# A hybrid decoder layer: token-major convolution products, and a state space that begins later and takes some steps on neighbouring weight pieces

## The chip, the cores and the metric

The kernel runs on one core of a Trainium2 chip. The metric is the device time of one execution in microseconds (us), the lower the better. An execution of the kernel before takes 1211.44 us (median of 3 runs, 1211.16 to 1211.69).

## The reference

One layer of a decoder with three mixers and a gated merge, for 256 tokens and a model width of 2048, all in float32:

```python
h = rms_norm(x, norm_w)
sb_q, sb_k, sb_v, sb_z, ssd_z, ssd_xbc, ssd_dt, mem_q, mem_z, gate_pre = split(h @ w_in)
o_sb  = stick_breaking_attention(sb_q, sb_k, sb_v) * silu(sb_z)
xbc   = silu(causal_depthwise_conv(ssd_xbc, conv_w, conv_b))     # 4096 channels, 4 taps
x_ssm, b_in, c_in = split(xbc)                                   # 2048, 1024, 1024
dt    = softplus(ssd_dt + dt_bias)
y     = ssd_chunked_scan(x_ssm, dt, -exp(a_log), b_in, c_in)     # 8 groups of 4 heads
o_ssd = group_rms_norm((y + d_skip * x_ssm) * silu(ssd_z))
o_mem = memory_cross_attention(mem_q, rms_norm(mem), w_mem_kv) * silu(mem_z)
gates = sigmoid(gate_pre + b_gate)
merged = g_sb * (o_sb @ w_branch_sb) + g_ssd * (o_ssd @ w_branch_ssd) + g_mem * (o_mem @ w_branch_mem)
out = rms_norm(x + merged @ w_out, final_norm_w)
```

## The kernel before

**Weight pieces.** All large products go through `gemm` (L249) or `gemm_cols` (L211). Weights are read once, in pieces of 512 KB (a tile `raw`, loaded by SyncE's queue). `split` (L142) makes two fp32r tiles of a piece: ScalarE (ACT) copies it to `wh` (L146), and VectorE (DVE) writes the rest, `wl = raw - wh` (L150). Three products in fp32r stand for one in fp32: high x high, high x low, low x high. There are three `wh` and three `wl` buffers, so the copy of a piece may start when TensorE (PE) has finished the piece three before it. In `gemm` a piece is 12 matmuls, 512 columns wide (L269 to L271), and the result lies token-major in PSUM, 128 tokens to a tile. In `gemm_cols` a piece is 8 matmuls 512 wide (L229, the high weights on both halves of the input at once) and 8 of 256 (L233), and the result lies channel-major.

**Side work.** After each piece `pump` (L185) issues the rest of the kernel: first the steps whose due piece has come (`defer`), then one step of one of two lanes, the even pieces' or the odd pieces'. A step is a Python generator's stretch up to its next `yield`. Every engine runs its instructions in the order in which they were issued, so what `pump` issues after piece n stands ahead of piece n+1's `wh` on ACT, ahead of its `wl` on DVE, and ahead of its matmuls on PE. Pieces are numbered here from the first: values, keys and queries of the memory attention, the z parts and the stick-breaking attention take 1 to 160, the convolution 161 to 224, the gates and projection of branch mem 225 to 272, of branch sb 273 to 320, of branch ssd 321 to 384, the output 385 to 408.

**Results turned by DVE.** Most products of `gemm` are wanted channel-major. `turning` (L301) does it: DVE transposes 32x32 blocks out of PSUM (L308), a DMA takes them to a scratch in DRAM (L313), four DMAs bring them back (L323), and ACT copies the blocks to their place.

**The convolution** (L733 on) uses `gemm_cols`, 16 calls of 4 pieces. `fold` (L239) adds the two halves of the result (ACT L246, DVE L247). Then `taps` does the four taps on DVE: a scaled copy (L745) and three scalar-tensor-tensor operations (L748, STT below). `silu` (L202) is one ACT operation of 128x1024 for four channel tiles. `turn_x` (L755 on) turns x token-major through a scratch again (DVE L764, DMAs L768 and L772), a quarter (two groups) at a time.

**The state space** (`ssd_group`, L813) has 8 groups, the even ones in one lane, the odd ones in the other. It is put into the lanes 4 pieces after the convolution (L933) and runs under the pieces of branches mem and sb. A group's steps are: the decay input by DMA and the products `cb` (PE L825, L826); `xs`, `cbs` (ACT L841) and the masked decays (DVE L844); 6 exponentials of 128x128 (ACT L851); 6 more, and a weighing by `cbs` (DVE L855); two weighings; the products `y` of two groups together (PE L874); the skip and z (DVE L887, L890); the squares (ACT L892), their split, their sum `tot` (PE L900); Ln, Exp, Identity, Square on ACT (L906 to L909); the scaling. After a wait of the lanes the result is split (`ssd_cols`). `finish` (L978) issues whatever is left in the lanes ahead of the first product of branch ssd.

**ACT's function tables.** Exponential and logarithm share one table (`exp_ln`, L804), sigmoid has another (the gates, `sigmoid`, L808), silu a third. `sigmoid` marks the table as gone, so that the next exponential loads it again.

**Gates and branches.** In each branch, for each of four column groups, first the gate's product (8 pieces), then the projection (4 pieces in branches mem and sb, 8 in branch ssd). `gate_evac` adds the bias on DVE (L951) and defers the sigmoid by one piece; `branch_evac` multiplies (L960, L962) and adds on GpSimd (POOL, L963).

Of the kernel before, what the change touches and what calls it, by code (L numbers as in the profile page):

```python
# [10 lines left out]
F32 = mybir.dt.float32  # L11
# [5 lines left out]
P = 128  # L17
# [24 lines left out]
def trunk_kernel(  # L42
# [159 lines left out]
    def silu(a, chunks=LATE):  # L202
        defer(lambda: nc.scalar.activation(a, a, AF.Silu), chunks)
# [529 lines left out]

    cT = [slot([P, 8, T], F32, "cT") for _ in range(4)]

    def conv_evac(i0):
        def evac(acc):
            u = tmp.tile([P, 2, T], F32, tag="cu", name=nm("cu"), bufs=2)
            fold(u, acc)
            for b in range(2):  # L740
                defer(lambda b=b: taps(u[:, b], i0 + b), 1 + 2 * b)

        def taps(u, i):
            a = cT[i // 8][:, i % 8]
            nc.vector.tensor_scalar(a, u, convw[:, 3, i:i + 1], convb[:, i:i + 1], ALU.mult,  # L745
                                    ALU.add)
            for s in range(1, 4):
                nc.vector.scalar_tensor_tensor(a[:, s:T], u[:, 0:T - s],  # L748
                                               convw[:, 3 - s, i:i + 1], a[:, s:T],
                                               ALU.mult, ALU.add)  # L750
# [33 lines left out]
    waiting = [zT[i // 2][:, 4 * (i % 2):4 * (i % 2) + 4] for i in range(4)]
    for i, g in enumerate((4, 5, 6, 7, 0, 1, 2, 3)):
        for j in range(2):
            gemm_cols(hT, NKT, w_in, C_XBC + g * GW + 2 * j * P, conv_evac(4 * g + 2 * j))
        waiting.insert(5 if i == 4 else len(waiting),
                       cT[g // 2][:, 4 * (g % 2):4 * (g % 2) + 4])
        if i >= 4:  # L790
            for j in range(3):
                silu(waiting.pop(0), 6 if not waiting else 1 + j)
        if i == 5:
            defer(lambda: turn_x(0), 5)


    oD = []
    ssd_done = []
    pair = []

    def exp_ln():

        if not tables[0]:
            nc.scalar.preload_act_table_set("natural_log_exp_and_others")  # L804
            tables[0] = True

    def sigmoid(a):
        nc.scalar.activation(a, a, AF.Sigmoid)  # L808
        tables[0] = False

    tables = [False]

    def ssd_group(g):  # L813

        heads = range(4 * g, 4 * g + 4)
        xT = [cT[i // 8][:, i % 8] for i in (2 * g, 2 * g + 1)]
        zg = turned(zT[g // 4], 2 * (g % 4), 2)

# [6 lines left out]
        nc.tensor.matmul(cb[:, 0:2], bT[:, g, 0:P], cTT[:, g], start=True, stop=True)  # L825
        nc.tensor.matmul(cb[:, 2], bT[:, g, P:T], cTT[:, g, P:T], start=True, stop=True)  # L826
        yield
        xs = tb([P, 2, T], "xs")
        rows = x_rows[g // 2]
        for t in range(2):  # L830
            for b in range(2):
                dt2 = dts[:, t, heads[0] + 2 * b:heads[0] + 2 * b + 2]
                nc.vector.tensor_tensor(
                    xs[:, t, b * P:(b + 1) * P].rearrange("p (h i c) -> p h i c", h=2, c=32),
                    rows[:, :, t, 2 * (g % 2) + b].rearrange("p (h i) c -> p h i c", h=2),
                    dt2.unsqueeze(2).unsqueeze(3).to_broadcast([P, 2, 2, 32]), ALU.mult)
# [4 lines left out]
        nc.scalar.activation(cbs, cb, AF.Copy)  # L841
        over = lambda a: a.unsqueeze(1).to_broadcast([P, 4, P])
# [277 lines left out]
```

## Time and profile before

| | |
|---|---|
| median of 3 runs | 1211.44 us |
| the profiled execution | 1211.59 us |
| its span in the trace | 1209.9 us |
| share of the span that PE is busy | 99% (5820 matmuls) |
| DVE, ACT, POOL | 65%, 52%, 4% |
| DMA share in the stretch 469 to 659 us (convolution) | 0.66 |
| granted TensorE clock, mean | 0.998 |

The span is the stretch of the trace from the first to the last instruction; the execution's time is 1.7 us longer. In rows of the timeline the first number is the start in us from the span's beginning, the second the duration; "x3" means that three instructions alike, one behind the other, were put into one row, and brackets at a row's end give the idle time ahead of it and what ended it. Durations of neighbours overlap a little, so what an instruction costs its engine is best read as the distance between two starts.

### The profile page before, as it was taken

The page shows a single profiled execution, that of the slowest core. Times are in us where ns is not written, and L with a number is a line of the kernel's source. Part 1 is how long each engine was busy: PE and PEld are TensorE (multiplying, and loading weights), DVE is VectorE, ACT ScalarE, POOL GpSimd, SP SyncE. Part 2 cuts the span into 40 slices and gives each one's busy share as a digit, 9 for nine tenths or more (in the row PEclk, how much of TensorE's full clock was granted, in tenths as well). Part 3 has the DMA queues.
Part 4 walks back from the last instruction along what each step waited for, and adds up shares of the span by engine and source line. Part 5 has one row for each costly group of instructions (what it writes and reads, how often), then busy time and mean ns, then how long its engine had stood idle before and what let it go on. Part 6 is the DMA issues. An engine that isn't in the chain of part 4 may idle for free.

```text
span 1209.9 us, 15621 instructions
## 1 busy us (share of the span) xinstructions
PE 1199.0 (99%) x5820; PEld 1005.8 (83%) x5820; DVE 791.6 (65%) x1035; ACT 634.1 (52%) x844; POOL 52.5 (4%) x50
## 2 busy tenths in 40 slices
PE   9999999999999999999999999999999999999997
PEld 7888888888888888888888888888888888888886
DVE  5686664546564555888887858677777655556752
ACT  6754443354355444545655756484757534444541
POOL 0100000000000000010100000000000010110101
PEclk9999999999999999999999999999999999999999
DMA  9977787887666777665668676667756677778751
GB/s 320 363 229 228 215 244 235 251 232 214 197 192 194 218 224 226 185 189 169 180 179 261 210 226 214 212 204 220 229 177 202 204 221 222 228 219 293 252 203 70
DMA packets 169820, 264.66 MB, mean 219 GB/s; under 512 B 11984, under 2 KB 67472, under 8 KB 169616
## 3 DMA queue, kind: packets, MB, share of 16 engines
q1 hardware_dynamic: 134304, 227.41, 61.6%
q10 hardware_dynamic: 35440, 36.26, 9.2%
q8 instruction: 45, 0.74, 0.2%
q14 instruction: 31, 0.25, 0.1%
HBM read 249.45 MB, written 14.19 MB: 218 GB/s over the span
## 4 chain that ended last, share of the span: by engine, by line
PE 97%; issue 1%; DMA 1%; ACT 0%; DVE 0%; SPq 0%; POOLq 0%; POOL 0%; ACTq 0%
PE acc L269 25%; PE acc L271 25%; PE acc L270 25%; PE acc L229 10%; PE acc L233 5%; PE acc L457 1%; PE acc L458 1%; PE acc L456 1%; PE y L874 1%; DMA raw<-in_w_mem_kv_dram 1%; PE dtp L518 0%; PE acc L1074 0%; PE acc L1072 0%; PE acc L1073 0%; PE spo L708 0%
## 5 line engine op out<-in xcount | busy, mean ns | idle before, releaser
L150 DVE TENSOR_TENSOR wl<-raw,wh 128x1024 fp32r<-128x1024 f32 (+1 forms) x409 | 504.4, 1236 | 309.4 <-ACT wh L146 307.9
L146 ACT ACTIVATE wh<-raw 128x1024 fp32r<-128x1024 f32 (+1 forms) x409 | 431.4, 1056 | 426.8 <-PE acc L271 337.1
L269 PE MATMUL acc<-wh,hT 128*128 128x512 f32 x896 | 350.9, 392 | 0.0
L270 PE MATMUL acc<-wl,hT 128*128 128x512 f32 x896 | 348.9, 389 | 0.3 <-DVE wl L150 0.3
L271 PE MATMUL acc<-wh,hT 128*128 128x512 f32 x896 | 348.9, 389 | 0.0
L271 PEld LDWEIGHTS acc<-wh,hT 128*128 128x128 f32 x896 | 168.2, 188 | 35.4
L270 PEld LDWEIGHTS acc<-wl,hT 128*128 128x128 f32 x896 | 168.3, 188 | 34.4 <-DVE wl L150 0.7
L269 PEld LDWEIGHTS acc<-wh,hT 128*128 128x128 f32 x896 | 168.3, 188 | 33.9 <-issue 0.3
L229 PE MATMUL acc<-hT,wh 128*128 128x512 f32 x512 | 161.6, 397 | 0.0
L233 PEld LDWEIGHTS acc<-hT,wl 128*128 128x128 f32 x512 | 96.2, 188 | 22.7
L233 PE MATMUL acc<-hT,wl 128*128 128x256 f32 x512 | 100.7, 278 | 0.0
L229 PEld LDWEIGHTS acc<-hT,wh 128*128 128x128 f32 x512 | 78.1, 189 | 0.1
L269 PE MATMUL acc<-wh,oD 128*128 128x512 f32 x128 | 49.8, 389 | 0.0
L270 PE MATMUL acc<-wl,oD 128*128 128x512 f32 x128 | 49.8, 389 | 0.0
L271 PE MATMUL acc<-wh,oD 128*128 128x512 f32 x128 | 49.8, 389 | 0.0
L748 DVE SCALAR_TENSOR_TENSOR cT<-cu,wcols,cT 128x255 f32<-128x255 f32 (+2 forms) x96 | 46.4, 483 | 3.4
L963 POOL TENSOR_TENSOR merged<-merged,sig 128x512 f32<-128x512 f32 x16 | 25.8, 1637 | 512.3 <-DVE sig L962 512.3
L269 PE MATMUL acc<-wh,mT 128*128 128x512 f32 x96 | 37.4, 390 | 0.0
L271 PE MATMUL acc<-wh,mT 128*128 128x512 f32 x96 | 37.4, 389 | 0.0
L270 PE MATMUL acc<-wl,mT 128*128 128x512 f32 x96 | 37.4, 389 | 0.0
L689 POOL TENSOR_TENSOR lm<-lm,sp 128x384 f32<-128x384 f32 x8 | 11.5, 1433 | 391.6 <-DVE sp L688 389.5
L269 PEld LDWEIGHTS acc<-wh,oD 128*128 128x128 f32 x128 | 24.0, 188 | 5.0
(243 smaller groups left out, 1298.8 us busy)
## 6 DMA issues: line engine op xcount, KB each, us to landing
raw<-in_w_in_dram SPq DMA_DIRECT2D x288, 512.0 KB, 4.4
raw<-in_w_branch_ssd_dram SPq DMA_DIRECT2D x32, 512.0 KB, 4.9
raw<-in_w_mem_kv_dram SPq DMA_DIRECT2D x31, 512.0 KB, 6.0
raw<-in_w_out_dram SPq DMA_DIRECT2D x24, 512.0 KB, 5.6
scratch<-blocks ACTq DMA_DIRECT2D x23, 512.0 KB, 4.2
raw<-in_w_branch_mem_dram SPq DMA_DIRECT2D x16, 512.0 KB, 4.9
raw<-in_w_branch_sb_dram SPq DMA_DIRECT2D x16, 512.0 KB, 5.0
turned<-scratch ACTq DMA_DIRECT2D x60, 128.0 KB, 4.6
```

The lines of the kernel that those rows point to most:

```text
L146: nc.scalar.activation(hi, src, AF.Copy, **({} if scale is None else {"scale": scale}))
L150: nc.vector.tensor_tensor(lo, src, h32, ALU.subtract)
L229: nc.tensor.matmul(halves[b], wh[:, kt - k0, b * P:(b + 1) * P], lhs.both(kt), start=first, stop=False, skip_group_check=True)
L233: nc.tensor.matmul(halves[b][:, 1], wl[:, kt - k0, b * P:(b + 1) * P], lhs.at(kt)[0], start=False, stop=last, skip_group_check=True)
L269: nc.tensor.matmul(a, lh[:, tt], wh[:, j], start=first, stop=False)
L270: nc.tensor.matmul(a, lh[:, tt], wl[:, j], start=False, stop=False)
L271: nc.tensor.matmul(a, ll[:, tt], wh[:, j], start=False, stop=last)
L456: nc.tensor.matmul(a, lh[:, tt], wh[:, g], start=first, stop=False)
L457: nc.tensor.matmul(a, lh[:, tt], wl[:, g], start=False, stop=False)
L458: nc.tensor.matmul(a, ll[:, tt], wh[:, g], start=False, stop=last)
L748: nc.vector.scalar_tensor_tensor(a[:, s:T], u[:, 0:T - s], convw[:, 3 - s, i:i + 1], a[:, s:T], ALU.mult, ALU.add)
L963: nc.gpsimd.tensor_tensor(merged[t][:, cs], merged[t][:, cs], sig[:, t], ALU.add)
```

## The change

- The convolution's products go through `gemm` and are turned by `turning`, 8 calls of 8 pieces. `fold` is gone. When the turned columns are back, ACT copies them into two tiles `cu`, and the taps of the four channel tiles follow 2 pieces apart (5 in the last call, `i0 == 12`, which is x's last quarter). The first tap is now on ACT (Identity with scale and bias); the three STT stay on DVE.
- The silus of the channels of B, C and z stay single ACT operations between the products. Those of x are done for quarters 0 and 1 when the taps are (`conv_done`); quarters 2 and 3 wait for a gate: behind its sigmoid, with the same table, ACT makes the sigmoid of two halves of 128x512 (`silu_late`, one buffer `sl`), and POOL multiplies.
- The first two groups take x by 4 PE transposes each (`xp`) in place of the scratch.
- The state space is put into the lanes 12 pieces after the convolution, not 4. From then on both lanes step at every piece whose number is a multiple of 8 (`faster`), so that one lane steps at pieces n-1, n and n+1.
- In branch ssd, gates 0 and 1 come first, then `finish`, then projections 0 and 1, gate 2, projection 2, gate 3, projection 3.

```diff
+    faster = []
     def pump():
...
         advance(lanes[now[0] % 2])
+        if faster and now[0] % 8 == 0:
+            advance(lanes[1 - now[0] % 2])
...
-    def conv_evac(i0):
-        def evac(acc):
-            u = tmp.tile([P, 2, T], F32, tag="cu", name=nm("cu"), bufs=2)
-            fold(u, acc)
-            for b in range(2):
-                defer(lambda b=b: taps(u[:, b], i0 + b), 1 + 2 * b)
+    def conv(i0):
+        pace = 5 if i0 == 12 else 2
+        def use(cols):
+            for k in (0, 2):
+                u = tmp.tile([P, 2, T], F32, tag="cu", name=nm("cu"), bufs=2)
+                nc.scalar.activation(blocked(u), tiles(cols, k, 2), AF.Copy)
+                for b in range(2):
+                    defer(lambda u=u, i=k + b: taps(u[:, i % 2], i0 + i),
+                          1 + pace * (k + b))
+            if i0 < 16:
+                defer(lambda: conv_done(i0 // 4), 2 + 3 * pace)
         def taps(u, i):
             a = cT[i // 8][:, i % 8]
-            nc.vector.tensor_scalar(a, u, convw[:, 3, i:i + 1], convb[:, i:i + 1], ALU.mult,
-                                    ALU.add)
+            nc.scalar.activation(a, u, AF.Identity, scale=convw[:, 3, i:i + 1],
+                                 bias=convb[:, i:i + 1])
             for s in range(1, 4):
...
+    def silu_late():
+        g = waiting.pop(0)
+        for k in range(4 * (g % 2), 4 * (g % 2) + 4, 2):
+            a = cT[g // 2][:, k:k + 2]
+            r = tmp.tile([P, 2, T], F32, tag="sl", name=nm("sl"), bufs=1)
+            nc.scalar.activation(r, a, AF.Sigmoid)
+            nc.gpsimd.tensor_tensor(a, a, r, ALU.mult)
+        silu_done.add(g)
...
+        gemm(hT, NKT, w_in, C_XBC + g * GW, conv(4 * g))
...
     def sigmoid(a):
         nc.scalar.activation(a, a, AF.Sigmoid)
+        if waiting:
+            silu_late()
         tables[0] = False
...
+        xp = None if g >= 2 else bank([P, 2, T], "xp")
+                    nc.tensor.transpose(xp[:, t, b * P:(b + 1) * P],
+                                        xT[b][:, t * P:(t + 1) * P], ident)
...
     def start_ssd():
+        faster.append(True)
...
-    defer(start_ssd, 4)
+    defer(start_ssd, 12)
...
+            for gate in ((0, 1), (), (2,), (3,))[g] if br == 2 else (g,):
```

PE has 5572 matmuls in place of 5820 (256 fewer in the convolution, 8 transposes more), and ACT has 24 table loads in place of 21.

**ACT, the first exponentials of the state space.** `cbs<-cb` is the copy of a `cb` product, `wh<-raw` the copy of the next weight piece, `dec` the decays; each `wh` row closes what one `pump` issued. Before:

```order
L841 ACTIVATE cbs_5697<-cb_5640 128x384
L146 ACTIVATE wh_5703<-raw_5701 128x1024
L841 ACTIVATE cbs_5727<-cb_5670 128x384
L146 ACTIVATE wh_5733<-raw_5731 128x1024
L804 ACT_TABLE_LOAD
L851 ACTIVATE dec_5636<-dec_5636,nacx 128x128 x4
L851 ACTIVATE dec_5635<-dec_5635,nac 128x128 x2
L146 ACTIVATE wh_5760<-raw_5758 128x1024
L851 ACTIVATE dec_5666<-dec_5666,nacx 128x128 x4
L851 ACTIVATE dec_5665<-dec_5665,nac 128x128 x2
L146 ACTIVATE wh_5785<-raw_5783 128x1024
L851 ACTIVATE dec_5635<-dec_5635,nac 128x128 x2
L851 ACTIVATE dec_5637<-dec_5637,nac 128x128 x4
L146 ACTIVATE wh_5811<-raw_5809 128x1024
```

Now:

```order
L888 ACTIVATE cbs_5658<-cb_5598 128x384
L146 ACTIVATE wh_5664<-raw_5662 128x1024
L801 ACT_TABLE_LOAD
L898 ACTIVATE dec_5551<-dec_5551,nacx 128x128 x4
L898 ACTIVATE dec_5550<-dec_5550,nac 128x128 x2
L898 ACTIVATE dec_5589<-dec_5589,nacx 128x128 x4
L898 ACTIVATE dec_5588<-dec_5588,nac 128x128 x2
L146 ACTIVATE wh_5696<-raw_5694 128x1024
L898 ACTIVATE dec_5588<-dec_5588,nac 128x128 x2
L898 ACTIVATE dec_5590<-dec_5590,nac 128x128 x4
L146 ACTIVATE wh_5722<-raw_5720 128x1024
L898 ACTIVATE dec_5550<-dec_5550,nac 128x128 x2
```

The table load had the 6 exponentials of one lane behind it ahead of the next `wh`, and the other lane's came a piece later; now the load and 12 exponentials, both lanes' (this is piece 240, a multiple of 8), stand ahead of one `wh`.

**ACT, a gate's sigmoid.** `sig` is a gate, `sl` the sigmoid of a late silu. Before, at a gate of branch mem, with the exponentials some pieces behind it:

```order
L808 ACT_TABLE_LOAD
L808 ACTIVATE sig_6451<-sig_6451 128x1024
L948 DMA sig_6747<-in_b_gate_dram 128x512
L146 ACTIVATE wh_6752<-raw_6750 128x1024
L146 ACTIVATE wh_6781<-raw_6779 128x1024
L841 ACTIVATE cbs_6802<-cb_6744 128x384
L146 ACTIVATE wh_6808<-raw_6806 128x1024
L841 ACTIVATE cbs_6834<-cb_6776 128x384
L146 ACTIVATE wh_6840<-raw_6838 128x1024
L804 ACT_TABLE_LOAD
L851 ACTIVATE dec_6740<-dec_6740,nacx 128x128 x4
L851 ACTIVATE dec_6739<-dec_6739,nac 128x128 x2
```

Now, first at piece 260, then at piece 284 (two stretches of ACT's order, the second 55 rows on):

```order
L146 ACTIVATE wh_6195<-raw_6193 128x1024
L805 ACT_TABLE_LOAD
L805 ACTIVATE sig_5910<-sig_5910 128x1024
L780 ACTIVATE sl_6212<-cT_3777 128x512
L780 ACTIVATE sl_6215<-cT_3777 128x512
L888 ACTIVATE cbs_6226<-cb_6163 128x384
L996 DMA sig_6230<-in_b_gate_dram 128x512
L146 ACTIVATE wh_6235<-raw_6233 128x1024
```

```order
L146 ACTIVATE wh_6806<-raw_6804 128x1024
L805 ACT_TABLE_LOAD
L805 ACTIVATE sig_6521<-sig_6521 128x1024
L801 ACT_TABLE_LOAD
L898 ACTIVATE dec_6712<-dec_6712,nacx 128x128 x4
L898 ACTIVATE dec_6711<-dec_6711,nac 128x128 x2
```

The gate's table load and sigmoid had a `wh` right behind them. At piece 260 they now have both late sigmoids and a `cbs` behind them ahead of the next `wh`; at piece 284 the exponentials' table load and 6 exponentials.

**DVE, the skip behind a pair of `y` products.** `wl` is the low part of a weight piece, `cT<-cT,wcols,y` the skip (two tiles), `zT` the gating; the groups are 6 and 7. On PE the 48 matmuls of both `y` stand, before, directly ahead of the products with the first `wl` here; now directly behind them, which is still ahead of those with the second. Before:

```order
L150 TENSOR_TENSOR wl_7051<-raw_7048,wh_7050 128x1024
L887 SCALAR_TENSOR_TENSOR cT_3777<-cT_3777,wcols,y_7001 128x256 x2
L890 TENSOR_TENSOR zT_3073<-zT_3073,cT_3777 128x2x8x32
L150 TENSOR_TENSOR wl_7077<-raw_7074,wh_7076 128x1024
L887 SCALAR_TENSOR_TENSOR cT_3777<-cT_3777,wcols,y_7023 128x256 x2
L890 TENSOR_TENSOR zT_3073<-zT_3073,cT_3777 128x2x8x32
L150 TENSOR_TENSOR wl_7099<-raw_7096,wh_7098 128x1024
```

Now, at piece 312:

```order
L150 TENSOR_TENSOR wl_7494<-raw_7491,wh_7493 128x1024
L934 SCALAR_TENSOR_TENSOR cT_3777<-cT_3777,wcols,y_7400 128x256 x2
L937 TENSOR_TENSOR zT_3073<-zT_3073,cT_3777 128x2x8x32
L150 TENSOR_TENSOR wl_7540<-raw_7537,wh_7539 128x1024
L940 TENSOR_TENSOR xs_7239<-xs_7239 128x256
L150 TENSOR_TENSOR wl_7560<-raw_7557,wh_7559 128x1024
L934 SCALAR_TENSOR_TENSOR cT_3777<-cT_3777,wcols,y_7509 128x256 x2
L937 TENSOR_TENSOR zT_3073<-zT_3073,cT_3777 128x2x8x32
L150 TENSOR_TENSOR wl_7581<-raw_7578,wh_7580 128x1024
```

The skip that waits for `y` had the low part of the next piece ahead of it on DVE; now it stands ahead of that low part, since at piece 312 one lane issues `y` and the other the skip in the same `pump`.

More of the change, by code (lines that the diff above doesn't have):

```diff
@@ L750, in taps, with conv_done, exp_ln, sigmoid @@
                                                ALU.mult, ALU.add)
-        return evac
+        return turning(use)
+    silu_done = set()
+    tables = [False]
+    def conv_done(g):
+        if g > 1:
+            waiting.append(g)
+            return
+        a = cT[g // 2][:, 4 * (g % 2):4 * (g % 2) + 4]
+        nc.scalar.activation(a, a, AF.Silu)
+        silu_done.add(g)
[6 more added lines that the diff above has]
+            nc.gpsimd.tensor_tensor(a, a, r, ALU.mult)
+        silu_done.add(g)
+    waiting = [zT[i // 2][:, 4 * (i % 2):4 * (i % 2) + 4] for i in range(4)]
+    for i, g in enumerate((4, 5, 6, 7, 0, 1, 2, 3)):
+        gemm(hT, NKT, w_in, C_XBC + g * GW, conv(4 * g))
+        if g >= 4:
+            waiting.append(cT[g // 2][:, 4 * (g % 2):4 * (g % 2) + 4])
+        else:
+            for j in range(min(3, len(waiting))):
+                silu(waiting.pop(0), 1 + j)
+    oD = []
+    ssd_done = []
+    pair = []
+    def exp_ln():
+        if not tables[0]:
+            nc.scalar.preload_act_table_set("natural_log_exp_and_others")
+            tables[0] = True
+    def sigmoid(a):
+        nc.scalar.activation(a, a, AF.Sigmoid)
+        if waiting:
+            silu_late()
+        tables[0] = False
+    def turn_when(m):
+        if m in silu_done:
+            turn_x(m)
+        else:
+            defer(lambda: turn_when(m), 1)
     x_rows = {}
@@ L782, in turn_x @@
             defer(lambda j=j: back(j), 8 + j)
[L784 to L811, printed above, removed]
     def ssd_group(g):
         heads = range(4 * g, 4 * g + 4)
+        assert g // 2 in silu_done, g
         xT = [cT[i // 8][:, i % 8] for i in (2 * g, 2 * g + 1)]
@@ L822, in ssd_group @@
             nc.sync.dma_start(dec[j], acT[j, h0:h0 + 4].partition_broadcast(P))
+        xp = None if g >= 2 else bank([P, 2, T], "xp")
+        for b in range(2):
+            for t in range(2):
+                if xp is not None:
+                    nc.tensor.transpose(xp[:, t, b * P:(b + 1) * P],
+                                        xT[b][:, t * P:(t + 1) * P], ident)
         cb = bank([P, 3, P], "cb")
@@ L828, in ssd_group @@
         xs = tb([P, 2, T], "xs")
[L829 to L836, printed above, removed]
+        by_head = lambda a: a.rearrange("p t (h c) -> p t h c", c=64)
+        if xp is not None:
+            nc.vector.tensor_tensor(by_head(xs), by_head(xp), dts[:, :, heads[0]:heads[0] + 4]
+                                    .unsqueeze(3).to_broadcast([P, 2, 4, 64]), ALU.mult)
+        else:
+            rows = x_rows[g // 2]
+            for t in range(2):
+                for b in range(2):
+                    dt2 = dts[:, t, heads[0] + 2 * b:heads[0] + 2 * b + 2]
+                    nc.vector.tensor_tensor(
+                        xs[:, t, b * P:(b + 1) * P].rearrange("p (h i c) -> p h i c", h=2, c=32),
+                        rows[:, :, t, 2 * (g % 2) + b].rearrange("p (h i) c -> p h i c", h=2),
+                        dt2.unsqueeze(2).unsqueeze(3).to_broadcast([P, 2, 2, 32]), ALU.mult)
         x_used.append(g)
         if len(x_used) % 2 == 0 and len(x_used) < SSD_GROUPS:
-            turn_x(len(x_used) // 2)
+            turn_when(len(x_used) // 2)
         cbs = small2([P, 3, P], "cbs")
@@ L973, in trunk_kernel @@
     for br, (g0, src, nk, wb) in enumerate(branches):
+        sigs = {}
         for g in range(4):
-            sig = t4([P, 2, GW], "sig")
-            gemm(hT, NKT, w_in, C_GATE + g0 + g * GW, gate_evac(g0 + g * GW, sig))
+            for gate in ((0, 1), (), (2,), (3,))[g] if br == 2 else (g,):
+                sigs[gate] = t4([P, 2, GW], "sig")
+                gemm(hT, NKT, w_in, C_GATE + g0 + gate * GW,
+                     gate_evac(g0 + gate * GW, sigs[gate]))
             if src is None:
@@ L980, in trunk_kernel @@
                 src = oD[0]
-            gemm(src, nk, wb, g * GW, branch_evac(br, g, sig))
+            gemm(src, nk, wb, g * GW, branch_evac(br, g, sigs[g]))
     yo = [slot([P, D], F32, "yo") for _ in range(2)]
```

## The prediction

> **What bounds the kernel now.** I read the page first, then the busy time by stretches, then the waits, and at last the timelines of the three engines that handle a weight piece. The page:
>
> ```profile
> span 1209.9 us, 15621 instructions
> PE 1199.0 (99%) x5820; PEld 1005.8 (83%) x5820; DVE 791.6 (65%) x1035; ACT 634.1 (52%) x844; POOL 52.5 (4%) x50
> PE 97%; issue 1%; DMA 1%; ACT 0%; DVE 0%; SPq 0%; POOLq 0%; POOL 0%; ACTq 0%
> ```
>
> PE is busy all the time and is 97% of the chain that ended last. Whatever shortens PE's own work is a gain; whatever else is added costs something only where it makes PE wait. Busy time by stretches (columns: PE, weight load, DVE, ACT, POOL, clock, DMA share, GB/s), first z and attention inputs, then the convolution:
>
> ```profile
> 75.00:339.00 264.00, 263.74 (x1221) 219.57 (x1220) 156.76 (x200) 122.00 (x144) 0.75 (x1) 1.00 0.76 227
> 469.00:659.00 190.00, 190.00 (x1096) 166.45 (x1096) 155.85 (x240) 101.53 (x122) 7.39 (x4) 1.00 0.66 194
> ```
>
> In the convolution PE is busy for all of 190 us at clock 1.00. In the waits of 660 to 960 us, where the state space runs, PE does not appear; ACT waits for PE before nearly every copy:
>
> ```profile
> ACT wh L146 <- PE acc L271: 75.4, 55, 2.0
> ACT cbs L841 <- PE cb L826: 12.8, 7, 2.3
> ACT wh L146 <- DMA raw<-in_w_branch_sb_dram: 2.5, 1, 2.5
> ```
>
> How far ahead are the copies? Rows of PE, ACT and DVE from a quiet place (branch ssd):
>
> ```profile
> 971.58 0.39 PE L269 MATMUL acc<-wh,oD 128*128 128x512 f32 x1
> 974.30 0.39 PE L269 MATMUL acc<-wh,oD 128*128 128x512 f32 x1
> 974.53 0.39 PE L270 MATMUL acc<-wl,oD 128*128 128x512 f32 x1
> 969.11 1.06 ACT L146 ACTIVATE wh<-raw 128x1024 fp32r<-128x1024 f32 x1 [1.66 <-PE acc L271]
> 970.20 1.23 DVE L150 TENSOR_TENSOR wl<-raw,wh 128x1024 fp32r<-128x1024 f32 x1 [1.50 <-ACT wh L146]
> ```
>
> A piece takes PE 2.72 us (971.58 to 974.30). The piece of 974.30 needs its `wl` at 974.53; its `wh` began at 969.11, 0.25 after PE left the piece three before (971.58 - 2.72 = 968.86), and its `wl` ended at 971.43. The cover is 974.53 - 971.43 = 3.10 us. So the rule of my sum: whatever ACT or DVE must do beyond 2.72 us per piece adds to a lag, shorter pieces take it back, and PE waits for what exceeds 3.10.
>
> **Part by part. The products: -4.4.** A convolution piece now is four groups of four matmuls; between these rows lie seven groups:
>
> ```profile
> 520.23 0.63 PE L229 MATMUL acc<-hT,wh 128*128 128x512 f32 x2
> 525.11 0.63 PE L229 MATMUL acc<-hT,wh 128*128 128x512 f32 x2
> ```
>
> 4.88 / 7 = 0.697 us a group, 2.789 a piece. Token-major it is a piece like that of 971.58, 2.72. The difference, 0.069, times 64 pieces is -4.4 us. The Trainium skill's page "TensorE: Matmul & The Clock Gate", section "Back-to-back issue gap", speaks against this: its isolated gap of N/2.4 + 2.5 ns would make it 2.600 against 2.590 a piece, a gain of 0.7 us in all by that estimate. The rows decide.
>
> **The x transposes: +0.9.** Eight transposes of 128x128 on PE, by a row of the chain:
>
> ```profile
> 1124.07 0.87 PE mt L943 x8
> ```
>
> **Off the path: 0.** The fold and the first tap leave DVE, 32 block transposes come to it; copies and first taps come to ACT; eight more megabytes go out to DRAM and back. The stretch 75 to 339 does the same turning with DVE at 59%, ACT at 46%, DMA at 0.76 and PE unwaiting; that is the cover. Without it, the nearest row above (a weight 2.5 us late, once) bounds it at +2.5; below nothing only if DMA pressure fell, which nothing suggests.
>
> **The state space in bunches: +6.4.** Where both lanes step, or a table load is put beside exponentials, the cover runs out. Prices on ACT:
>
> ```profile
> 673.79 1.05 ACT L146 ACTIVATE wh<-raw 128x1024 fp32r<-128x1024 f32 x1
> 674.86 1.28 ACT L804 ACT_TABLE_LOAD   x1
> 676.16 1.28 ACT L851 ACTIVATE dec<-dec,nacx 128x128 f32<-128x128 f32 x4
> 681.59 1.85 ACT L851 ACTIVATE dec<-dec,nac 128x128 f32<-128x128 f32 x6
> 683.34 1.04 ACT L146 ACTIVATE wh<-raw 128x1024 fp32r<-128x1024 f32 x1
> 684.29 1.85 ACT L851 ACTIVATE dec<-dec,nac 128x128 f32<-128x128 f32 x6
> 794.49 1.06 ACT L808 ACTIVATE sig<-sig 128x1024 f32<-128x1024 f32 x1
> 787.64 0.48 ACT L906 ACTIVATE xs<-tot,eps 128x256 f32<-128x256 f32 x1 [0.60 <-PE tot L900]
> 789.14 1.05 ACT L146 ACTIVATE wh<-raw 128x1024 fp32r<-128x1024 f32 x1
> 867.59 0.49 ACT L841 ACTIVATE cbs<-cb 128x384 f32<-128x384 f32 x1 [1.87 <-PE cb L826]
> 867.97 1.05 ACT L146 ACTIVATE wh<-raw 128x1024 fp32r<-128x1024 f32 x1
> 703.80 0.63 ACT L892 ACTIVATE xs<-zT 128x512 f32<-128x512 f32 x1 [2.11 <-DVE zT L890]
> ```
>
> By distances of starts: a `wh` 0.95, or 1.07 ahead of a load; a load 1.30; six exponentials 1.75; `cbs` 0.38; Ln to Square 1.50. The sigmoid is 1.06, and each half of a late silu 0.63 like 703.80. `wh` and six exponentials make 2.70: such a piece gives back nothing. PE's own part, DVE's and POOL's:
>
> ```profile
> 787.21 0.40 PE L900 MATMUL tot<-sq,rb 128*128 128x256 f32 x2
> 866.74 0.59 PE L825 MATMUL cb<-cT,cT 128*128 128x256 f32 x2
> 867.31 0.47 PE L269 MATMUL acc<-wh,oS 128*128 128x512 f32 x1
> 703.63 0.40 PE L270 MATMUL acc<-wl,hT 128*128 128x512 f32 x1
> 502.92 1.52 DVE L748 SCALAR_TENSOR_TENSOR cT<-cu,wcols,cT 128x255 f32<-128x255 f32 x3
> 504.36 0.42 DVE L678 SCALAR_TENSOR_TENSOR lm<-slg,smask 128x256 f32<-128x256 f32 x1
> 691.59 1.29 DVE L855 TENSOR_TENSOR dec<-dec,cbs 128x512 f32<-128x512 f32 x2
> 692.79 2.35 DVE L150 TENSOR_TENSOR wl<-raw,wh 128x1024 fp32r<-128x1024 f32 x2
> 702.11 0.87 DVE L887 SCALAR_TENSOR_TENSOR cT<-cT,wcols,y 128x256 f32<-128x256 f32 x2 [4.58 <-PE y L874]
> 703.62 1.22 DVE L150 TENSOR_TENSOR wl<-raw,wh 128x1024 fp32r<-128x1024 f32 x1
> L963 POOL TENSOR_TENSOR merged<-merged,sig 128x512 f32<-128x512 f32 x16 | 25.8, 1637 | 512.3 <-DVE sig L962 512.3
> L995 POOL TENSOR_TENSOR yo<-yo,fw 128x512 f32<-128x512 f32 x6 | 7.7, 1298 | 56.4 <-ACT junk L994 56.4
> ```
>
> - Piece 240: `cbs` leaves a lag of 867.97 - 867.31 - 0.25 = 0.41. Then `wh`, load and 12 exponentials: 1.07 + 1.30 + 3.50 - 2.72 = 3.15 more. 3.56 against 3.10: PE waits **0.45**.
> - Piece 244, on DVE: exponentials have kept the cover used up. Three STT 1.44 (502.92 to 504.36), two weighings 1.20, a `wl` 1.14: 3.78 - 2.72, **1.0**.
> - Piece 260: `cbs` after 256 waits for a `cb` of one piece before (two apart now), so the lag is 2.72 + 0.41; 257 and 259 keep it (six exponentials each), 258 gives back 2.72 - 1.06, and its `cb` 0.57 (866.74 to 867.31): 0.9 is left. Then 1.07 + 1.30 + 1.06 + 0.63 + POOL + 0.63 + 0.38 - 2.72 = 2.35 + POOL, since one buffer makes the second half wait for POOL's product, and ACT has the `cbs` and the next `wh` behind it. POOL takes 1.30 to 1.64: the lag is 4.5 to 4.9, the wait 1.4 to 1.8. Nothing in the rows decides between the two; I take **1.4**, the lower end, and keep 1.8 for the range.
> - Pieces 284 and 308: 1.07 + 1.30 + 1.06 + 1.30 + 1.75 - 2.72 = 3.76, **0.65** each.
> - Piece 297: Ln waits for a `tot` of one piece before, not two: 2.72 + (787.64 - 787.21) + 1.50 - 0.25 - 0.2 of PE's own = 4.2, **1.05**.
> - Piece 312: the skip, which waits for `y`, now stands ahead of the next `wl`. In the rows that `wl` would end at 703.62 + 1.22 = 704.84, and PE would want it at 703.63: **1.2**.
>
> At 250, the first late silu, no exponentials are near, and the table needs no second load: 0. The sum is 0.45 + 1.0 + 1.4 + 0.65 + 1.05 + 0.65 + 1.2 = 6.4. Each wait is what is left of 3.10 after much larger numbers; an error of 0.4 in each lag puts the sum between 3.6 and 9.2.
>
> Net: -4.4 + 0.9 + 6.4 = +2.9. Against the profiled execution, 1209.9 + 1.7 = 1211.59, this is 1214.5; that execution lies 0.15 above the median, so 1214.3.
>
> **The rivals.** About 0.2%, 2.4 us, is what a measurement of this kernel tells from no change.
>
> *The cover is a little deeper.* The excesses of 0.45 and 0.65 vanish and the larger ones shrink: waits of 3 to 3.5. For it speaks that ACT runs ahead on every quiet piece, against it that the 3.10 comes from such a piece. -4.4 + 0.9 + 3.2: 1211.2.
>
> *No new wait at all, only the shorter products*: the other side. Place: the 64 pieces; price -4.4 + 0.9. It decides if bunched steps are absorbed by pieces in hand, that is, if each lag stays under 3.10. Against it: the lags at 260, 297 and 312 each pass it by over 1 us. 1208.0.
>
> *Weights come late on top.* With the cover spent, a transfer like that of 2.5 us (the row of branch sb), or POOL at 1.64, lands on PE. The scratch traffic now stands in branch mem's start too. Another 2.5 to 3: 1217.2.
>
> *Table loads cost double.* In the rows the next activation starts 1.30 after a load's start (674.86, 676.16); were another 1.38 paid, the six loads at 240, 260, 284 and 308 would add 8.3: 1222.6. The Trainium skill's page "ScalarE: Activation LUTs", section "What ACT_TABLE_LOAD costs", states such a drain of about 1380 ns behind the 1283 ns of the load. By that rule this rival would hold; the trace agrees with 1283 and shows no drain.
>
> **How the numbers follow.** The forecast, waits near 6: 0.46, of which 0.08 falls within 0.2%; its own range is 1212.0 to 1216.5. The deeper cover: 0.28, within. No wait: 0.12, faster. Late weights: 0.12, slower. The drain: 0.02, slower. Faster 0.12, same 0.28 + 0.08 = 0.36, slower 0.38 + 0.12 + 0.02 = 0.52. The range leaves out no wait, the drain and a little of late weights: 1210.2 to 1217.5.
>
> **What would show it.** Right: L269 in the convolution at 2.72 a piece, no L229 and L233; PE waiting for `wl` L150 in seven places between 240 and 313 with 0.4 to 1.5 us each, and nowhere else. A single wait over 2 us, or waits in the convolution, would make the third rival right; PE's convolution pieces at 2.78 would make the first term wrong; waits under 2 us in all would put the time under 1210.

## The result, and the profile after

| | before | changed |
|---|---|---|
| median | 1211.41 us (6 runs, 1211.16 to 1212.45) | 1218.70 us (6 runs, 1217.69 to 1219.78) |
| profiled execution | 1211.59 us | 1218.29 us |
| its span | 1209.9 us | 1216.5 us |

The ratio is 1.0057 (95% interval 1.0046 to 1.0067): slower by 7.3 us, where +2.9 was forecast and 1217.5 was the upper end. The page of the changed kernel:

```profile
span 1216.5 us, 15190 instructions
PE 1199.1 (99%) x5572; PEld 993.8 (82%) x5572; DVE 779.7 (64%) x993; ACT 654.2 (54%) x881; POOL 58.7 (5%) x54
PE 92%; DVE 3%; ACT 2%; issue 2%; DMA 1%; SPq 0%; POOLq 0%; POOL 0%; ACTq 0%; DVEq 0%
```

PE's share of the chain fell from 97% to 92%; DVE and ACT, at 0% before, have 5% of it. The busy time of PE does not show the gain of the shorter products: a matmul's end in the rows is modelled, so part of a wait counts as busy. Where the time went is read from the starts. First the convolution, from its first product to the first product behind it, of the kernel before:

```profile
469.74 0.39 PE L229 MATMUL acc<-hT,wh 128*128 128x512 f32 x1
...
658.25 0.40 PE L269 MATMUL acc<-wh,hT 128*128 128x512 f32 x1
```

and of the changed kernel:

```profile
469.92 0.39 PE L272 MATMUL acc<-wh,hT 128*128 128x512 f32 x1
...
654.52 0.39 PE L272 MATMUL acc<-wh,hT 128*128 128x512 f32 x1
```

188.51 against 184.60 us: the products gave 3.9 us, and PE waits nowhere in between. Everything else was lost behind it. The waits of PE between 660 and 960 us in the changed kernel (before there was none):

```profile
PE acc L273 <- DVE wl L150: 6.0, 8, 1.5
```

The timeline of PE has the places; at the first, the matmul ahead and the one behind are shown too:

```profile
700.32 0.39 PE L272 MATMUL acc<-wh,hT 128*128 128x512 f32 x1
700.95 0.50 PE L273 MATMUL acc<-wl,hT 128*128 128x512 f32 x1 [0.24 <-DVE wl L150]
701.28 0.39 PE L274 MATMUL acc<-wh,hT 128*128 128x512 f32 x1
...
712.80 0.50 PE L273 MATMUL acc<-wl,oM 128*128 128x512 f32 x1 [0.60 <-DVE wl L150]
...
763.52 0.50 PE L273 MATMUL acc<-wl,hT 128*128 128x512 f32 x1 [1.50 <-DVE wl L150]
...
834.50 0.50 PE L273 MATMUL acc<-wl,hT 128*128 128x512 f32 x1 [0.53 <-DVE wl L150]
...
874.35 0.50 PE L273 MATMUL acc<-wl,hT 128*128 128x512 f32 x1 [0.76 <-DVE wl L150]
...
881.11 0.50 PE L273 MATMUL acc<-wl,hT 128*128 128x512 f32 x1
...
907.11 0.50 PE L273 MATMUL acc<-wl,hT 128*128 128x512 f32 x1 [0.53 <-DVE wl L150]
...
922.38 0.50 PE L273 MATMUL acc<-wl,hT 128*128 128x512 f32 x1 [1.10 <-DVE wl L150]
...
956.61 0.50 PE L273 MATMUL acc<-wl,hT 128*128 128x512 f32 x1 [0.78 <-DVE wl L150]
```

Two matmuls of this kind are 0.227 us apart when nothing waits (2.72 / 12). From 700.32 to 700.95 are 0.63, from there to 701.28 are 0.33: this place costs 0.40 + 0.11 = 0.51 us, though its row gives only 0.24 as idle. Read so, from the starts, the nine places cost:

| next products | forecast, at piece | measured |
|---|---|---|
| 700.95 | 0.45 (240) | 0.51 |
| 712.80 | 1.0 (244) | 0.87 |
| 763.52 | 1.4 (260) | 2.14 |
| 834.50 | 0.65 (284) | 0.80 |
| 874.35 | 1.05 (297) | 1.14 |
| 881.11 | none | 0.43 |
| 907.11 | 0.65 (308) | 0.80 |
| 922.38 | 1.2 (312) | 1.26 |
| 956.61 | none | 1.05 |
| sum | 6.4 | 9.0 |

-3.9 + 0.9 + 9.0 = 6.0 of the 6.7 us between the profiled executions; 0.2 more lie ahead of the convolution, the other 0.5 are spread too thin to place. (What is issued behind piece 240 shows as a wait in piece 241, and so on; the forecast named the first, the waits are named below by either.) Two places, in pieces 300 and 325, were not forecast, and 260 was too low. Look at DVE there. The changed kernel at piece 260, first ACT, then DVE, then POOL:

```profile
757.39 0.62 ACT L780 ACTIVATE sl<-cT 128x512 f32<-128x512 f32 x1
759.50 0.63 ACT L780 ACTIVATE sl<-cT 128x512 f32<-128x512 f32 x1 [1.50 <-POOL cT L781]
...
760.42 1.99 ACT L146 ACTIVATE wh<-raw 128x1024 fp32r<-128x1024 f32 x2
758.04 1.99 DVE L880 TENSOR_TENSOR xs<-turned,dts 128x128 f32<-128x128 f32 x4
759.95 2.38 DVE L891 TENSOR_TENSOR dec<-dec,cmask 128x512 f32<-128x512 f32 x2
762.25 1.21 DVE L150 TENSOR_TENSOR wl<-raw,wh 128x1024 fp32r<-128x1024 f32 x1
758.08 1.39 POOL L781 TENSOR_TENSOR cT<-cT,sl 128x512 f32<-128x512 f32 x1 [34.31 <-ACT sl L780]
760.21 1.57 POOL L781 TENSOR_TENSOR cT<-cT,sl 128x512 f32<-128x512 f32 x1 [0.74 <-ACT sl L780]
```

ACT waits 1.5 us for POOL, as forecast, and its copy `wh` starts at 760.42. But DVE ends its masks only at 762.33 and makes the `wl` after that: DVE ends last, not ACT. And ahead of the wait at 956.61, under POOL's adds of branch sb, first POOL, then DVE:

```profile
949.62 3.53 POOL L1011 TENSOR_TENSOR merged<-merged,sig 128x512 f32<-128x512 f32 x2 [34.84 <-ACT oD L146]
949.66 2.34 DVE L150 TENSOR_TENSOR wl<-raw,wh 128x1024 fp32r<-128x1024 f32 x1
951.93 1.51 DVE L958 TENSOR_TENSOR xs<-xs,cbs 128x256 f32<-128x256 f32 x1
```

A `wl`, else 1.23, takes 2.34 while POOL works. The kernel before has such a row too, under POOL's adds (here DVE, then POOL), and PE did not wait there:

```profile
840.63 2.31 DVE L150 TENSOR_TENSOR wl<-raw,wh 128x1024 fp32r<-128x1024 f32 x1
839.13 2.73 POOL L963 TENSOR_TENSOR merged<-merged,sig 128x512 f32<-128x512 f32 x2 [257.43 <-DVE sig L962]
```

These rows made a second theory: POOL's work is not free for DVE.

### The profile page after: what moved, and what is told of

Its sections match the earlier page's. It is cut to its first block, busy times and chain, and to the rows that moved or that the text cites. A ratio compares the mean times of both kernels' runs of the same rounds, so it can differ in the third digit from the quotient of the medians.

```text
span 1216.5 us, 15190 instructions
## 1 busy us (share of the span) xinstructions
PE 1199.1 (99%) x5572; PEld 993.8 (82%) x5572; DVE 779.7 (64%) x993; ACT 654.2 (54%) x881; POOL 58.7 (5%) x54
## 4 chain that ended last, share of the span: by engine, by line
PE 92%; DVE 3%; ACT 2%; issue 2%; DMA 1%; SPq 0%; POOLq 0%; POOL 0%; ACTq 0%; DVEq 0%
PE acc L273 28%; PE acc L274 28%; PE acc L272 28%; DVE wl L150 2%; PE acc L460 1%; PE acc L461 1%; PE acc L459 1%; ACT wh L146 1%; PE y L921 1%; ACT dec L898 1%; DMA raw<-in_w_mem_kv_dram 1%; PE dtp L521 0%; PE acc L1125 0%; PE acc L1124 0%; PE acc L1123 0%
## 5 line engine op out<-in xcount | busy, mean ns | idle before, releaser
L273 PE MATMUL acc<-wl,hT 128*128 128x512 f32 x1152 | 449.5, 390 | 5.8 <-DVE wl L150 5.7
L272 PE MATMUL acc<-wh,hT 128*128 128x512 f32 x1152 | 451.9, 392 | 0.1
L274 PE MATMUL acc<-wh,hT 128*128 128x512 f32 x1152 | 448.7, 390 | 0.0
L273 PEld LDWEIGHTS acc<-wl,hT 128*128 128x128 f32 x1152 | 216.4, 188 | 52.3 <-DVE wl L150 9.1
L274 PEld LDWEIGHTS acc<-wh,hT 128*128 128x128 f32 x1152 | 216.3, 188 | 45.3
L272 PEld LDWEIGHTS acc<-wh,hT 128*128 128x128 f32 x1152 | 216.4, 188 | 44.1 <-ACT wh L146 0.8
L311 DVE STREAM_TRANSPOSE blocks<-acc 128x512 f32<-128x512 f32 x48 | 31.4, 691 | 0.0
L272 PEld LDWEIGHTS acc<-wh,oD 128*128 128x128 f32 x128 | 24.0, 188 | 5.0
L274 PEld LDWEIGHTS acc<-wh,oD 128*128 128x128 f32 x128 | 24.0, 188 | 5.0
L273 PEld LDWEIGHTS acc<-wl,oD 128*128 128x128 f32 x128 | 24.0, 188 | 4.9
L459 PE MATMUL acc<-wh,memT 128*128 128x512 f32 x64 | 25.2, 394 | 1.5 <-ACT memT L146 1.5
```

The source lines that it names most:

```text
L272: nc.tensor.matmul(a, lh[:, tt], wh[:, j], start=first, stop=False)
L273: nc.tensor.matmul(a, lh[:, tt], wl[:, j], start=False, stop=False)
L274: nc.tensor.matmul(a, ll[:, tt], wh[:, j], start=False, stop=last)
L311: nc.vector.transpose(blocks[:, t].rearrange("p j k c -> p k j c"), rows[t].rearrange("p (k j c) -> p k j c", k=4, j=4))
L459: nc.tensor.matmul(a, lh[:, tt], wh[:, g], start=first, stop=False)
```

## The experiments

In the expectations, theory A is that the waits come from bunched steps, B that they are ACT's alone, C that late transfers cause them, D that they come from where the steps fall among the gates, E that the turned convolution causes them.

**One lane a piece.** The bunching is taken out of the changed kernel:

```diff
     def start_ssd():
-        faster.append(True)
```

> Undoes one part: only one lane steps at every piece. Theory A (the waits come from steps that were bunched, 9.0 us of waits in the changed kernel): the waits at pieces 240, 244, 284, 297, 308, 312 and 325 go; left is the late silu at 260 with the exponentials' table load two pieces on, 1.5 to 2.5 us. 1211.4 - 3.9 + 0.9 + 2.0 = 1210.4 us. Theory C (late transfers from the added scratch traffic cause the waits): the traffic is the same, so the waits stay and the time is above 1215 us.

Measured: 1219.66 us, ratio 1.0067 (1.0054 to 1.0079). No gain, if anything 1 us worse than with the bunches, so theory A as I put it falls. PE's waits are now at 261, 285, 288, 309, 312 and 326. PE at 288 and 312, and POOL and DVE at 288:

```profile
842.67 0.50 PE L273 MATMUL acc<-wl,hT 128*128 128x512 f32 x1 [2.02 <-DVE wl L150]
...
916.33 0.57 PE L273 MATMUL acc<-wl,hT 128*128 128x512 f32 x1 [2.01 <-DVE wl L150]
838.55 2.98 POOL L1010 TENSOR_TENSOR merged<-merged,sig 128x512 f32<-128x512 f32 x2 [79.96 <-DMA raw<-in_w_in_dram]
838.94 1.46 DVE L902 TENSOR_TENSOR dec<-dec,cbs 128x512 f32<-128x512 f32 x1
840.32 2.29 DVE L150 TENSOR_TENSOR wl<-raw,wh 128x1024 fp32r<-128x1024 f32 x1
```

POOL's two adds stand on a weighing (0.65 alone) and a `wl` again. And the two waits, alike in size, did not cost the same. Busy time by stretches of 3.41 us, two at each wait; behind the length come PE, weight load, DVE, ACT and POOL, then the clock:

```profile
838.13:841.54 3.41, 2.52 (x12) 1.73 (x10) 3.41 (x4) 2.81 (x3) 2.98 (x2) 1.00 0.85 194
841.54:844.96 3.41, 2.29 (x10) 1.91 (x11) 3.41 (x5) 0.03 (x1) 0.00 (x0) 1.00 0.60 181
...
913.22:916.63 3.41, 1.40 (x6) 0.86 (x6) 3.41 (x4) 1.06 (x1) 1.37 (x1) 1.00 0.24 92
916.63:920.04 3.41, 3.41 (x9) 2.64 (x8) 1.92 (x2) 0.00 (x0) 0.00 (x0) 0.50 0.73 215
```

Behind the second the granted clock was 0.50, and PE made 9 matmuls in 3.41 us, where 15 fit at full clock.

**POOL's work on DVE.**

```diff
-            nc.gpsimd.tensor_tensor(a, a, r, ALU.mult)
+            nc.vector.tensor_tensor(a, a, r, ALU.mult)
...
-                    nc.gpsimd.tensor_tensor(merged[t][:, cs], merged[t][:, cs], sig[:, t],
+                    nc.vector.tensor_tensor(merged[t][:, cs], merged[t][:, cs], sig[:, t],
```

> The late silus' multiplies and the merge's adds are on DVE, not on POOL. Theory A with a second cause (while POOL works, DVE's instructions stand still about 1.1 us per POOL instruction): the DVE rows of 1.5 to 2.4 us near 260, 299 and 323 go back to 0.4 to 1.3; the waits at 300 (0.4) and 325 (1.05) go, that at 260 falls from 2.1 to 1.0 to 1.6: about 1216.4 us. Theory B (the waits are ACT's alone, as forecast): DVE has 0.6 us more to do for each add: not faster, 1218.7 us or more.

Measured: 1218.02 us, ratio 1.0052 (1.0039 to 1.0066). The interval does not separate this from the changed kernel, and the 1216.4 that the second cause expected was missed. The places tell more: a new wait of 0.9 came at 249, where DVE's multiply of the first late silu now lies; near 300 the wait fell to 0.1, near 325 to 0.3, as the second cause asks; at 260 it stayed (2.0 us from the starts, 2.14 in the changed kernel), since ACT now waits for DVE's multiply. The rows of xs and masks:

```profile
761.67 0.89 DVE L880 TENSOR_TENSOR xs<-turned,dts 128x128 f32<-128x128 f32 x4
762.48 1.29 DVE L891 TENSOR_TENSOR dec<-dec,cmask 128x512 f32<-128x512 f32 x2
```

are back to 0.89 and 1.29. My size for 260 was wrong, the durations right; theory B, by which this could not lower any wait, does not hold for 300 and 325.

**Two buffers for the late sigmoid.**

```diff
-            r = tmp.tile([P, 2, T], F32, tag="sl", name=nm("sl"), bufs=1)
+            r = tmp.tile([P, 2, T], F32, tag="sl", name=nm("sl"), bufs=2)
```

> Two buffers for the late silu's sigmoid, so that ACT's second half does not wait for POOL. Theory B: the wait at 260 falls by the 1.4 us that ACT no longer waits, 1217.3 us. Theory A with POOL holding DVE: DVE still ends its masked decays at the same time, the wait at 260 stays within 0.4 us of 2.1: 1218.5 us.

Measured: 1218.67 us, ratio 1.0058 (1.0044 to 1.0072): no gain, as the second cause said. ACT no longer waits, but DVE loses as much to POOL as before, and PE's idle time is not shorter:

```profile
757.70 2.71 POOL L781 TENSOR_TENSOR cT<-cT,sl 128x512 f32<-128x512 f32 x2 [35.72 <-ACT sl L780]
757.65 3.10 DVE L880 TENSOR_TENSOR xs<-turned,dts 128x128 f32<-128x128 f32 x4
763.15 0.51 PE L273 MATMUL acc<-wl,hT 128*128 128x512 f32 x1 [1.92 <-DVE wl L150]
```

```profile
763.00:767.00 4.00, 3.85 (x10) 3.06 (x11) 4.00 (x7) 1.82 (x4) 0.00 (x0) 0.57 0.50 137
```

Four xs products take 3.10 us for 0.89: all of POOL's 2.71 lies on them. The second fence, of the busy time by stretches, again has a low clock (0.57) behind the wait; without it the place would cost 2.2 us, as in the changed kernel. ACT's wait for POOL, which the forecast priced, was hidden behind DVE's.

**The late multiply left out.** Quarters 2 and 3 of x go on without their silu.

```diff
-            nc.gpsimd.tensor_tensor(a, a, r, ALU.mult)
```

> Leaves out the multiply of the late silus, so quarters 2 and 3 of x go on without their silu. Theory A with POOL holding DVE: at 260 the four xs products take 0.9 us again and the two masks 1.3 (2.0 and 2.4 in the changed kernel), and the wait falls from 2.1 to about 0.3: 1216.9 us. Theory B: the same wait falls since ACT has nothing to wait for, but the DVE durations stay as they are in the changed kernel.

Measured: 1215.67 us, ratio 1.0033 (1.0021 to 1.0045). PE no longer waits at 260, and DVE has its usual durations:

```profile
758.19 0.89 DVE L879 TENSOR_TENSOR xs<-turned,dts 128x128 f32<-128x128 f32 x4
758.99 1.29 DVE L890 TENSOR_TENSOR dec<-dec,cmask 128x512 f32<-128x512 f32 x2
```

With POOL silent DVE needs 0.89 + 1.29 = 2.18 for what took 1.99 + 2.38 = 4.37 beside two POOL instructions: 1.1 us for each. The time fell 3.0 us, 1.2 more than expected and 0.9 more than the wait at 260; between the profiled executions it is 2.5, and the wait near 325 was also 0.3 shorter here. This shows POOL's hold on DVE with nothing else changed in the order. It does not price it alone, since ACT's wait for POOL went too; the run with two buffers took only that wait away and gained nothing.

**The later start alone.** The kernel before, with its channel-major convolution, all its silus and one lane a piece:

```diff
-    defer(start_ssd, 4)
+    defer(start_ssd, 12)
```

(and branch ssd's gates in the changed order).

> The kernel before with the state space alone begun 8 pieces later (and the gates of branch ssd in the changed order, so that it can end at piece 332); convolution, silus and lanes as before. Theory D (what costs is where the state space's steps fall among the gates, whose sigmoid, multiplies and POOL adds come every 12 pieces): the waits that the one-lane kernel has at 285 (1.2), 288 (2.3), 309 (1.2), 312 (2.3 and a stretch of low clock) and 326 (0.7) come here too, 7.5 to 9.5 us: 1220 us. Theory E (the turned convolution and its late silus cause the waits, the later start is harmless): 1211.4 us.

Measured: 1221.53 us, ratio 1.0080 (1.0067 to 1.0093). The start alone costs 10 us, with the old convolution. The waits of PE from 660 to 960 us:

```profile
PE acc L270 <- DVE wl L150: 5.5, 4, 2.0
```

The one at 288 in the timeline, and the `wl` ahead of it, which again stood beside POOL's adds:

```profile
844.04 0.50 PE L270 MATMUL acc<-wl,hT 128*128 128x512 f32 x1 [1.99 <-DVE wl L150]
841.70 2.29 DVE L150 TENSOR_TENSOR wl<-raw,wh 128x1024 fp32r<-128x1024 f32 x1
```

The waits stand at 285, 288, 309 and 312, where the one-lane kernel has them, with the same sizes to 0.2 us; at 326, where 0.7 was expected, it is 0.4 from the starts. Theory E falls, D holds.

**Twelve later in place of eight.** The same kernel, begun one whole gate period (8 pieces of gate, 4 of projection) later than before:

```diff
-    defer(start_ssd, 4)
+    defer(start_ssd, 16)
```

> The kernel before with the state space begun 12 pieces later, one whole period of the gates (8 later cost 10 us in the run of that). Theory D: as the kernel before but for one meeting with POOL's adds near 288, 1.4 to 2 us: 1213.0 us. If lateness itself cost, it would be above 1221 us.

Measured: 1213.36 us, ratio 1.0010 (1.0001 to 1.0019). Four pieces later still than the run that lost 10 us, and only 1.4 us are lost, at the one place foreseen:

```profile
842.28 0.50 PE L270 MATMUL acc<-wl,hT 128*128 128x512 f32 x1 [1.31 <-DVE wl L150]
```

**The token-major convolution with the old phase.** Three kernels of the changed convolution with one lane a piece, begun at piece 240. In the first, all silus of x by ACT's own silu:

```diff
-        if g > 1:
-            waiting.append(g)
-            return
...
-        faster.append(True)
...
-    defer(start_ssd, 12)
+    defer(start_ssd, 16)
```

> Token-major convolution, one lane a piece, all silus of x by ACT's own silu, and the state space begun 16 pieces after the convolution: 12 later than in the kernel before, one whole period of the gates. Theory D: the steps meet the gates as they do in the kernel before; left are 0.5 us near 245 and up to 1.4 near 288 (POOL's adds hold DVE): 1211.4 - 3.9 + 0.9 + 2.0 = 1210.4 us, at best 1209. If only the mere lateness counted, it would be slower than the start 8 pieces later, above 1219 us.

Measured: 1211.60 us, ratio 0.9999 (0.9990 to 1.0008): 7 us under the changed kernel, though it starts later; 1.2 us above the expectation. Where PE waits in it is not shown. In the second, POOL's adds are on DVE as above:

> As the run before it in this call, with the merge's adds on DVE in place of POOL. If POOL's adds hold DVE longer than DVE needs for them itself (1.1 against 0.6 us each), the wait near 288 falls from 1.4 to 0.9: 1209.9 us, 0.5 below that run. If POOL's work is free for DVE, it is slower than that run by up to 1 us.

Measured: 1211.48 us, ratio 1.0000 (0.9991 to 1.0009). The two are not told apart, and this one is 1.6 us above its expectation. From the starts PE waits 0.9 us at 250 and 1.2 at 288, elsewhere 0.4 at most. In the third, the late silus and POOL are as in the changed kernel:

> As the first start-240 run, but with the late silus as in the changed kernel (sigmoid behind the gate's, POOL's multiply). Tells what the late silus cost in an order that else waits little: with POOL's multiplies holding DVE near 248 and 260 another 3.5 to 4 us, 1214.3 us; if they are hidden behind the sigmoid as intended, 1210.4 us.

Measured: 1215.25 us, ratio 1.0030 (1.0019 to 1.0042). The late silus cost 3.6 us more than ACT's own silu with its table loads. At 288, with the adds on POOL, PE waits 1.6 us, 0.4 more than with the adds on DVE. Near 250, ACT and DVE both come late, one after the other, and the clock falls:

```profile
723.02 0.50 PE L272 MATMUL acc<-wh,hT 128*128 128x512 f32 x1 [1.06 <-ACT wh L146]
...
724.50 0.56 PE L273 MATMUL acc<-wl,hT 128*128 128x512 f32 x1 [0.98 <-DVE wl L150]
```

```profile
725.00:727.50 2.50, 2.50 (x8) 1.94 (x7) 2.46 (x5) 0.36 (x1) 0.00 (x0) 0.50 0.69 205
```

**The old start with the new convolution.** One lane, late silus kept, `defer(start_ssd, 4)`.

> The changed kernel with one lane a piece and the state space begun where the kernel before begins it (late silus kept). Theory D: the steps meet the gates as before, but now the last taps, the copies of the turned convolution and the late silus lie on them: 3 to 4 us of waits near 230 to 262, none later: 1211.4 - 3.9 + 0.9 + 3.5 = 1211.9 us. If a late start were harmless and an early one not, it would be above 1219 us.

Measured: 1213.37 us, ratio 1.0011 (1.0002 to 1.0019): 1.5 above the expectation, and 5.3 below the changed kernel. From 264 on PE waits nowhere; what is left lies where the last taps, the copies and the first late silu meet the first steps, most of it at 236 (1.3 us from the starts) and 249 (1.1). So the start had a reason to move, but not to 236.

**Spread out.** The second of the three kernels above (begun at 240, one lane a piece, ACT's own silu, adds on DVE), and each step that still met another moved:

```diff
-        pace = 5 if i0 == 12 else 2
+        pace = 4 if i0 == 12 else 2
...
-        xp = None if g >= 2 else bank([P, 2, T], "xp")
+        xp = None
...
-            turn_when(len(x_used) // 2)
+            defer(lambda m=len(x_used) // 2: turn_when(m), 5)
...
+                    plus = lambda t=t: nc.vector.tensor_tensor(
+                        merged[t][:, cs], merged[t][:, cs], sig[:, t], ALU.add)
+                    if br == 1:
+                        defer(plus, 2 + t * 0)
```

(`turn_x(0)` is called 5 pieces after the convolution, with a buffer of its own.)

> A version meant to beat both: as the start-240 run with adds on DVE, and each step that still met another is moved: the merge's adds of branch sb come 2 pieces after its multiplies, x's transposes 5 pieces later, the last taps 4 pieces apart, and the first two groups take x through the scratch (no PE transposes). Theory D: no wait over 0.4 us is left between 225 and 330: 1211.5 - 3.9 + 0.4 = 1208.0 us, down to 1207.3. If the waits come from something that the order does not decide, they stay: 1210 us or more.

Measured: 1208.89 us, ratio 0.9976 (0.9967 to 0.9985): 3.0 us faster than before, 9.8 faster than the changed kernel, 0.9 above the expectation. It beats both. The four moves were made together, so what each is worth is not shown. The waits of PE from 660 to 960 us:

```profile
PE acc L273 <- DVE wl L150: 0.2, 1, 0.2
```

From the starts there are three, of 0.4, 0.5 and 0.2 us, at 240, 248 and 266.

## Why the prediction was right in its sign and wrong in its size

**The products (-4.4): right, a little small.** Measured -3.9. In the 40 pieces without side work a piece shrank by 0.067 as forecast (0.069); in the other 24, side products split the row of matmuls and the gain was 0.035 to 0.07. The Trainium skill's isolated gap ("TensorE: Matmul & The Clock Gate", section "Back-to-back issue gap"), by which all of it would be, as an estimate, 0.6 us (64 times 2.600 - 2.590; the prediction has 0.7), does not fit the starts above.

**The x transposes (+0.9): right.** Pieces 236 and 237 are 0.44 and 0.45 us longer than their `cb` alone makes such pieces (1.01 and 1.13 against 0.57 and 0.68 over 2.72).

**Off the path (0): right** for the convolution, where PE does not wait.

**The state space (+6.4, measured 9.0): the step that failed.** Seven places were named, and seven were there; the six without 260 were forecast at 5.0 and measured 5.4: the cover of 3.10 us and the lags held. What failed is the bullet on piece 260, "2.35 + POOL": it let POOL's work count only where ACT waits for it, and POOL's adds of branch sb were put at nothing. The rows show that POOL's instructions also stop DVE, 1.1 us each at 260. There ACT's `wh` starts at 760.42, and a `wl` that starts 1.09 behind its `wh`, as at 969.11 and 970.20 in the prediction's rows, would have started at 761.51; it started at 762.25. Without these 0.74 us the wait of 2.14 would have been the 1.4 of the forecast. POOL's hold on DVE also adds 0.43 at 300 (DVE's first xs row there, else 0.42, takes 1.20 under POOL's adds) and 1.05 near 325, where the adds now fall on a DVE that has no slack. Together that is 2.2 of the 2.6 us by which the sum was too small. The rest of the way from 2.9 to 7.3 us is 0.5 of the products, 0.2 ahead of the convolution, 0.5 unplaced, and some 0.6 by which the profiled executions stand differently to their medians (0.4 below it here, 0.2 above it before). The runs of the changed kernel lie in two groups, 1217.7 to 1218.3 at a mean granted clock of 0.998 to 0.999 and 1219.1 to 1219.8 at 0.997. One stretch of low clock like that of the two-buffer kernel (3.41 us at half clock, some 1.6 us of time) takes 0.0014 off the mean, so it fits both differences; the only trace is of the first group, so at which wait it falls is not shown.

**"Bunches" was the wrong name for the cause.** Undoing the bunches made it 1 us worse, and the later start alone cost the old kernel 10 us. What decides is at which piece of the gates' period of 12 the state space's steps fall: 8 later they meet the sigmoid's table loads (285, 309) and POOL's adds (288, 312); 12 later they meet almost nothing. The bunches move steps off some of the worst places (the 2.3 us at 288 are not there with them); that they give back 1 us is within the intervals.

**The rivals.** The table loads did not cost double: behind the load at piece 240 (its start 693.77) the next exponential starts at 695.06, 1.29 later. Late weights were not it: from 660 to 960 us ACT waited for weights from DRAM twice,

```profile
ACT wh L146 <- DMA raw<-in_w_in_dram: 3.0, 2, 2.0
```

about as in the kernel before (once, 2.5 us), and PE's waits are gone in the spread kernel, which has no less scratch traffic. No new wait and a deeper cover are refuted by the nine places.

## What to carry to other kernels

Where one engine is the bound and the others keep a fixed lead on it, price a moved step by what else is issued in the same stretch: with work that comes in a period, a shift by a whole period cost 1.4 us here and a shift by two thirds of it 10 us. An engine with 4% of the span can still cost time, if its instructions stop another that is on the way to the bound; look whether rows of the same form have two durations, and what ran beside the long ones; the kernel before had such rows. Where steps meet others, moving them by a few pieces can be worth more than the shorter products: with one lane and the late silus kept, the state space begun 4 pieces later, at 240, was 4.4 us faster (1219.66 against 1215.25), and the products gave 3.9.

## What the runs showed of the hardware

**POOL stops DVE.** Beside a POOL add or multiply of 128x512, DVE instructions with both inputs in SBUF take 0.8 to 1.1 us more per POOL instruction (1.99 for 0.89, 2.34 for 1.23, 1.46 for 0.65). The Trainium skill's page "SBUF — State Buffer", section "Who interferes with whom", states that a DVE instruction with two SBUF inputs contends with a GpSimd instruction that reads SBUF, since DVE's second input comes through a read interface that both share. The trace agrees; the rule has no price, but it would have pointed at 260, 300 and 325.

**The clock falls after about 2 us of idle time, if they lie within one step of its record.** In three runs PE's starts were once 2.30 to 2.40 us apart (1.9 to 2.0 us idle), in a fourth 1.45 and 1.48 us one behind the other, and the seven to nine matmuls behind came 0.427 us apart, at a granted clock of 0.50 to 0.57 in the stretches shown. That costs about 1.6 us on top of the wait. The gap of 2.40 at 842.67 (piece 288) and its like at 844.04 in the kernel begun 8 later went without. The traces tell them apart. Their records of the clock have steps of 3.413 us: but for the last of a trace, every stretch of one clock is a whole number of them long, and the low stretches named here are one step each (916.63 to 920.04 in the one-lane kernel). In the four cases with a low clock the gap, or both gaps, lie whole in the step ahead, and PE is busy, as the rows model it, for 1.37 to 1.50 of its 3.41 us. The two gaps that went without are cut by the end of a step, with 2.52 and 2.29 us busy in the two steps of the one and 1.92 and 2.92 in those of the other. A gap of 2.11 us at 764.96 in the kernel with POOL's work on DVE lies in one step, leaves 1.70 us busy, and went without too; at the very start of the kernel without the multiply, a step with 1.70 us busy has a low one behind it. So in these traces the limit lies near 1.7 us busy, half a step, and where the steps fall differs from trace to trace. The Trainium skill's page "TensorE: Matmul & The Clock Gate", section "What's actually happening", has the low clock after an idle window of about 3.4 us; here a step of that length was enough of which PE was idle for more than half.
